# Rotated q and k as 16-bit halves, balanced by the norm weights; k transposed once, c spread by a transfer, and the list of instructions laid anew

## The chip, the cores and the metric

The kernel runs on one core of one Trainium2 chip. The metric is device time in microseconds (us) for one execution. The engines are named as the profile names them: PE (TensorE, with PEld for its weight loads), DVE (VectorE), ACT (ScalarE), POOL (GpSimd) and SP (SyncE, which here only issues transfers).

## The reference: one decoder layer with two mixers

The layer works on x (1 x 1024 x 1024, 32-bit). A conditioning row c gives shift, scale and gate; the normalised and modulated x goes through one input projection; its columns feed a sparse attention with three branches and a diagonal state-space mixer in parallel; both are gated, joined and projected back. Cut to what matters here:

```
mod = silu(c) @ w_ada + b_ada                       # shift, scale, gate
h = rms_norm(x, norm_g) * (1 + scale) + shift
q, kcr, vcr, ksl, vsl, kwn, vwn, z_a, g_br, u, z_s = split(h @ w_in)
q = rms_norm(q, q_norm_g)                           # 8 heads of 64
k_slc, k_win = rms_norm(ksl, k_slc_norm_g), rms_norm(kwn, k_win_norm_g)   # 2 groups of 64
q_r, k_slc, k_win = (apply_rope(v, cos, sin) for v in (q, k_slc, k_win))
# compressed branch: q (not rotated) against kc; selected and window branch:
s = einsum(q_r, k) * 64 ** -0.5;  p = masked_softmax(s);  o = p @ v
attn = (g0 * o_cmp + g1 * o_slc + g2 * o_win) * silu(z_a)
y = s5_mixer(u);  y = gelu(y);  ssm = y * sigmoid(y @ glu_w + glu_b) * silu(z_s)
out = x + gate * (concat(attn, ssm) @ w_out)
```

With 1024 positions and 16 selected blocks of 64, the selected branch takes all earlier keys; the window branch takes the last 512.

## The kernel before

**Recording and order.** The kernel first records every instruction under a short name and an engine letter, and then issues them in the order of a long list, `ORD`: `ha00:p5` means the next five PE instructions of the item `ha00` (letters p, v, a, g, s for PE, DVE, ACT, POOL, SP). Each engine keeps exactly this order, and takes its instructions strictly in turn. `SLOTS` gives each tile its buffer. All rows of the profile carry line L375, the helper that issues, so that instructions are told apart by their tiles.

**Start.** Row tiles of x are loaded, c is loaded as one row and spread over the 128 partitions by a matmul with ones (`sc_half`, line 528, tile `pcb`), SiLU is formed from it, and DVE multiplies and sums it with the rows of w_ada (`wada`, 24 times). DVE also forms the row norms, x is scaled, transposed by PE (`ptr`) and written as high and low part (`hhi`, `hlo`).

**Projections.** All products with 32-bit data are taken as three matmuls: high x high, high x low, low x high (`ptp` for k, v and q, `pcp` for the others).

**k.** `kv_norm` (line 768) normalises two row tiles of k, multiplies by the norm weights (`gains`) and by the rotary tables on DVE; `rope` (line 705) adds the halves on POOL and writes each head's 64 columns twice side by side (`kr`). `part2` (line 779) transposes the doubled heads on PE (`pkt`, 8 transposes for two row tiles), ACT copies the result (`kh`), and on the lower 64 partitions DVE subtracts it from the exact value: so the upper 64 rows hold k's high part and the lower 64 its low part. `kh` goes to DRAM (`kTd`) and comes back as `kT` (`kt`, line 1799), 128 partitions by 4 x 1024, 32 bits each.

**q.** `q_rope` doubles the rotated q in the same way; `q_trans` (line 1395) transposes it, ACT takes the high part `qh` (times 1/8), DVE the rest `ql`.

**Attention.** Blocks of 128 queries go in the order 0, 1, 2, 3, 7, 6, 5, 4, eight heads each. `head_a` (line 1452) takes the scores S of both branches: for `qh` and then `ql` as the stationary operand, kT streams through in pieces of up to 512 columns, so that the 128 rows sum high and low part of k; masks are added by a 16-bit matmul (`dmask`, `identb`). DVE finds the row maximum (`st`), ACT the exponential (`pp`); `head_b` on ACT writes the 16-bit high part of the weights (`hl`), `head_c` on DVE the low part, and SP's transposing transfer makes `PT`. `unit_b` multiplies PT by the values on PE (`po<-V,PT`, 64 columns each). In blocks 4 to 7 the selected branch has 640 to 1024 keys and the window branch 640; in blocks 0 to 3 both have 128 to 512.

**Beside it** PE has the state-space part, the gate projections (`pcp`), and behind them the output projection (`po<-wo`), which the list puts between the heads.

Of the kernel before, what the change touches and what calls it, by code (L numbers as in the profile page):

```python
# [75 lines left out]
cmpk:p2 tab0:v cmpk:p u3:a cmpk:p tab0:v cmpk:p qa0:p kpbn0:v scan0:v2 cmpk:p mats0:a u3:s cmpk:p2 tab1:v tab1:a cmpk:p
scan1:a cmpk:p2 scan0:a qa0:p2 mats0:a qa0:p scan0:v qa0:p2 mats1:p tab1:v mats1:p2 scan0:v mats1:p4 mats0:v mats1:p2
scan0:v mats1:p4 scan0:v mats1:p3 cmpk:p tab1:v cmpk:p2 mats1:a mats0:v cmpk:p tab1:v cmpk:p mats0:s mats1:a cmpk:p
mats1:p tab1:v mats0:s mats1:p3 scan0:v mats1:p3 mats1:a mats1:p mats0:s qa1:p scan0:v qa1:p mats1:a qa1:p2 xl2:s
mats1:a qa1:p2 mats0:s scan0:v cmpk:p mats1:a cmpk:p2 mats0:s mats1:a cmpk:p2 scan0:v cmpk:p mats0:s cmpk:p2 scan0:v  # L80
mats0:s scan1:p2 scan0:v scan1:p qaw4:s scan1:p scan0:v scan1:p mats0:s scan1:p2 scan0:v scan1:p scan1:a qaw3:s qa2:p2
scan1:a scan0:v qa2:p mats3:g qa2:p scan1:a qa2:p scan0:v qa2:p scan1:a cmpk:p scan1:v2 cmpk:p cmpk:a cmpk:p2 kpbn0:v
scan1:v cmpk:p2 cmpk:a cmpk:p cmpk:a scan1:v cmpk:p cmpk:a cmpk:p cmpk:a cmpk:p kpbn0:v cmpk:a scan0:v cmpk:p cmpk:a
cmpk:p cmpk:a cmpk:p kpbn0:v scan1:v cmpk:p3 scan1:v cmpk:p2 kpbn0:v qa0:p scan1:v qa0:p2 mats1:v qa0:p scan1:v qa0:p2
# [233 lines left out]
    pos="01",  # L318
# [1627 lines left out]
```

## Time and profile before

Three timed runs gave 638.22, 639.57 and 639.63 us. The profile is of one further execution.

| | |
|---|---|
| median of the timed runs | 639.57 us |
| time of the profiled execution | 643.35 us |
| its span, first to last instruction | 640.3 us |
| PE matmul busy | 604.2 us (94%) |
| PE weight loads busy | 488.4 us (76%) |
| DVE busy | 560.2 us (87%) |
| ACT busy | 377.6 us (59%) |
| POOL busy | 143.1 us (22%) |
| granted TensorE clock | 1.000 |

Busy time is the time in which at least one instruction of an engine is under way. Matmuls overlap each other, so a row's mean is longer than the time from one start to the next. A row of a group gives line, engine, operation, the tiles written and read, shapes, the count, then busy us and mean ns of one, then the idle time of the engine before them with what ended it. A row of the waits gives who waited for whom: us in total, times, longest. The timeline gives start, length, and what ran.

### The profile page before, as it was taken

The page shows a single profiled execution, that of the slowest core. Times are in us where ns is not written, and L with a number is a line of the kernel's source. Part 1 is how long each engine was busy: PE and PEld are TensorE (multiplying, and loading weights), DVE is VectorE, ACT ScalarE, POOL GpSimd, SP SyncE. Part 2 cuts the span into 40 slices and gives each one's busy share as a digit, 9 for nine tenths or more (in the row PEclk, how much of TensorE's full clock was granted, in tenths as well). Part 3 has the DMA queues.
Part 4 walks back from the last instruction along what each step waited for, and adds up shares of the span by engine and source line. Part 5 has one row for each costly group of instructions (what it writes and reads, how often), then busy time and mean ns, then how long its engine had stood idle before and what let it go on. Part 6 is the DMA issues. An engine that isn't in the chain of part 4 may idle for free.

```text
span 640.3 us, 12597 instructions
## 1 busy us (share of the span) xinstructions
PE 604.2 (94%) x4662; PEld 488.4 (76%) x4662; DVE 560.2 (87%) x1107; ACT 377.6 (59%) x732; POOL 143.1 (22%) x162
## 2 busy tenths in 40 slices
PE   2499999999999999999999999999999899999996
PEld 0388887888888887888888876657779788788884
DVE  5999988899878799898776879989999999999974
ACT  3596443755226325437677797786677677756750
POOL 1132225401873002170131011011120311201200
PEclk9999999999999999999999999999999999999999
DMA  8985325612869653063386979996999999999996
GB/s 316 398 311 119 100 66 162 190 39 50 219 166 279 187 133 101 18 168 126 99 161 166 171 161 240 175 221 219 204 205 179 221 209 215 238 218 239 234 174 197
DMA packets 209759, 116.75 MB, mean 182 GB/s; under 512 B 159073, under 2 KB 188513, under 8 KB 209698
## 3 DMA queue, kind: packets, MB, share of 16 engines
q1 hardware_dynamic: 205858, 109.38, 70.2%
q0 software_dynamic: 3840, 6.57, 4.7%
q8 instruction: 36, 0.59, 0.4%
q14 instruction: 25, 0.20, 0.1%
HBM read 58.10 MB, written 18.61 MB: 120 GB/s over the span
## 4 chain that ended last, share of the span: by engine, by line
PE 26%; DVE 11%; DMA 10%; issue 4%; ACT 3%; POOL 1%; SPq 0%; ACTq 0%; DVEq 0%; POOLq 0%
PE po L375 12%; PE S L375 6%; DMA PT<-hl 6%; PE pcp L375 5%; DVE hl L375 4%; DVE st L375 3%; DVE ps L375 1%; ACT pp L375 1%; DMA wor<-in_w_out_dram 1%; ACT hl L375 1%; DMA wr<-in_w_in_dram 1%; DMA yd<-Y 1%; DMA zz<-zsd 1%; PE pc L375 1%; POOL qr L375 1%
## 5 line engine op out<-in xcount | busy, mean ns | idle before, releaser
L375 ACT ACTIVATE pp<-S,st 128x640 f32<-128x640 f32 (+7 forms) x128 | 88.9, 698 | 48.0 <-DVE st L375 25.1
L375 ACT ACTIVATE hl<-pp,st 128x640 f16<-128x640 f32 (+7 forms) x128 | 90.0, 732 | 28.8 <-DVE st L375 13.1
L375 DVE SCALAR_TENSOR_TENSOR hl<-pp,st,hl 128x640 f16<-128x640 f32 (+7 forms) x128 | 97.6, 783 | 5.1 <-ACT hl L375 4.8
L375 DVE TENSOR_REDUCE st<-S 128x1 f32<-128x640 f32 (+7 forms) x96 | 84.3, 883 | 9.3 <-PE S L375 8.4
L375 PE MATMUL po<-wo,oh 128*128 128x512 f32 x264 | 83.6, 401 | 2.5 <-DVE ps L375 1.5
L375 PE MATMUL pcp<-hhi,wh 128*128 128x512 f32 x208 | 84.5, 406 | 0.4 <-DVE zz L375 0.2
L375 PE MATMUL ptp<-wsp,hhi 128*128 128x512 f32 x256 | 84.3, 410 | 0.0
L375 PE MATMUL pcp<-hlo,wh 128*128 128x512 f32 x208 | 82.3, 396 | 0.0
L375 PE MATMUL pcp<-hhi,wl 128*128 128x512 f32 x208 | 82.0, 394 | 0.0
L375 PE MATMUL S<-kT,qh 128*128 128x128 f32 (+3 forms) x192 | 60.8, 375 | 1.4 <-ACT pp L375 1.2
L375 PE MATMUL po<-V,PT 128*128 128x64 f16 x1584 | 58.6, 193 | 0.9 <-DMA PT<-hl 0.9
L375 PEld LDWEIGHTS po<-wo,oh 128*128 128x128 f32 x264 | 48.5, 188 | 14.3 <-ACT hl L375 1.8
L375 PEld LDWEIGHTS <-PT 128*128 128x128 f16 x1584 | 54.0, 98 | 3.5 <-issue 1.6
L375 PEld LDWEIGHTS ptp<-wsp,hhi 128*128 128x128 f32 x256 | 47.8, 193 | 10.6 <-issue 0.3
L375 PE MATMUL S<-kT,ql 128*128 128x128 f32 (+3 forms) x192 | 53.7, 338 | 0.0
L375 PE MATMUL ptp<-wsp,hlo 128*128 128x512 f32 x128 | 51.3, 402 | 0.0
L375 PE MATMUL po<-wo,ol 128*128 128x512 f32 x120 | 47.4, 395 | 0.0
L375 PEld LDWEIGHTS pcp<-hlo,wh 128*128 128x128 f32 x208 | 39.1, 188 | 9.3 <-issue 0.2
L375 PEld LDWEIGHTS pcp<-hhi,wh 128*128 128x128 f32 x208 | 39.2, 189 | 8.9 <-DVE zz L375 0.4
L375 PEld LDWEIGHTS pcp<-hhi,wl 128*128 128x128 f32 x208 | 39.2, 188 | 8.2 <-issue 0.2
L375 POOL TENSOR_TENSOR qr<-ropeb 128x512 f32<-128x512 f32 x16 | 21.8, 1381 | 96.3 <-DVE ropeb L375 56.1
L375 PEld LDWEIGHTS S<-kT,qh 128*128 128x128 f32 x192 | 33.2, 190 | 8.1 <-ACT pp L375 3.0
(310 smaller groups left out, 1264.2 us busy)
## 6 DMA issues: line engine op xcount, KB each, us to landing
wada<-in_w_adaT_dram SPq DMA_DIRECT2D x24, 512.0 KB, 6.8
wr<-in_w_in_dram SPq DMA_DIRECT2D x14, 512.0 KB, 5.2
x<-in_x_dram SPq DMA_DIRECT2D x8, 512.0 KB, 7.0
wor<-in_w_out_dram SPq DMA_DIRECT2D x8, 512.0 KB, 4.8
out_dram<-o SPq DMA_DIRECT2D x16, 256.0 KB, 2.8
wraw<-in_w_in_dram SPq DMA_DIRECT2D x15, 256.0 KB, 4.2
xo<-in_x_dram SPq DMA_DIRECT2D x14, 256.0 KB, 3.7
ud<-U SPq DMA_DIRECT2D x4, 512.0 KB, 3.3
```

Source lines behind the costliest of these rows:

```text
L375: op(*now(a), **{n: now(x) for n, x in k.items()})
```

## The change

- q's and k's rotated halves are written as 16-bit floats (F16) instead of 32-bit ones (F32R): `kh`, `kTd`, `kT`, `qh`, `ql`. The score matmuls keep their number and their columns.
- So that 16 bits hold them, `balance` measures the squares of the norm weights of q and k and multiplies one by a power of two and the other by its inverse: two ACT squares and a dozen small DVE operations on `gains`, ahead of all that uses them.
- `rope` writes k once instead of twice; `part2` transposes the plain heads (4 transposes for two row tiles), takes one copy (high) and one subtraction (low) over all 128 partitions, and stores both apart. `kt` puts high and low part on the upper and lower partitions as it loads.
- c is loaded by a transfer that writes its row to all 128 partitions; ones, `pcb` and their matmuls go.
- `ORD` and `SLOTS` are laid anew as a whole.

```
-prep0:g kvaw0:s xl_1:s s5l:s2 pre:s3 kvaw0:a pre:s2 kvaw0:g pre:s pre:v mb2:s s5p:v ma0:s sc0:p s5p:v2 lb:s s5p:v2 lb:s
...
-    cr = w4([1, 1024], F32, "cr")
-    dma(cr[:], t["c"].rearrange("(a d) -> a d", a=1))
+    cr = w4([128, 1024], F32, "cr")
+    dma(cr[:], t["c"].partition_broadcast(128))
...
-    ones = w2([1, 128], F32, "ones")
-    dve.memset(ones[:], 1.0)
...
-        pcb = ppv("pcb")
-        pe.matmul(pcb[:], ones[:], cr[:, halves(n)], start=True, stop=True)
-        act.activation(sc[:, halves(n)], pcb[:], AF.Tanh, scale=0.5)
-        stt(sc[:, halves(n)], sc[:, halves(n)], 1.0, pcb[:], OP.add, OP.mult)
+        act.activation(sc[:, halves(n)], cr[:, halves(n)], AF.Tanh, scale=0.5)
+        stt(sc[:, halves(n)], sc[:, halves(n)], 1.0, cr[:, halves(n)], OP.add, OP.mult)
...
+        balance(g)
         return cs, g
+
+    def balance(g):
+        junk = w2([128, 144], F32, "bj")
+        ss, v, w, n, f = (junk[:, 128 + 2 * k:130 + 2 * k] for k in range(5))
+        act.activation(junk[:, :64], g[:, 0, :], AF.Square, accum_out=ss[:, 0:1])
+        act.activation(junk[:, :128], g[:, 1:3, :].rearrange("p a d -> p (a d)"), AF.Square, accum_out=ss[:, 1:2])
+        ts(dve, v, ss.bitcast(I32), 2.0 ** -25, None, OP.mult)
+        for k, (top, off) in enumerate(((78.5, 1.0), (75.5, -1.0))):
+            ts(dve, w[:, k:k + 1], v[:, k:k + 1], -2.0, top, OP.mult, OP.add)
+            tt(dve, n[:, k:k + 1], v[:, 1 - k:2 - k], v[:, k:k + 1], OP.subtract)
+            stt(n[:, k:k + 1], n[:, k:k + 1], off, w[:, k:k + 1], OP.add, OP.min)
+        ts(dve, n, n, MAG, None, OP.add)
+        ts(dve, n, n, MAG, None, OP.subtract)
+        ts(dve, f.bitcast(I32), n, 8388608.0, 127.0 * 8388608.0, OP.mult, OP.add)
+        ts(dve, g[:, 0, :], g[:, 0, :], f[:, 0:1], None, OP.mult)
+        gk = g[:, 1:3, :].rearrange("p a d -> p (a d)")
+        ts(dve, gk, gk, f[:, 1:2], None, OP.mult)
...
         for h, op in ((0, OP.subtract), (1, OP.add)):
+            if m == 2:
+                tt(pool, o[:, :, 32 * h:32 * h + 32], c[:, :, h], b[:, :, 1 - h], op)
+                continue
...
-    kTd = dram.tile([128, 4, 1024], F32, name="kTd")
+    kTd = dram.tile([128, 2, 2, 1024], F16, name="kTd")
...
-        kr = w4([128, 8, 2, 64], F32, "kr")
+        kr = w4([128, 2, 8, 64], F32, "kr")[:, 0]
...
-            kh = w4([128, 4, 256], F32R, "kh")
-            for j in range(2):
-                pt = ppv("pkt")
-                for b in range(4):
-                    pe.transpose(pt[:, b * 128:(b + 1) * 128], kr[:, 4 * j + b].rearrange("p a d -> p (a d)"), ident[:])
-                pt4 = pt[:].rearrange("p (b t) -> p b t", b=4)
-                ks = kh[:, :, 128 * j:128 * j + 128]
-                act.copy(ks, pt4)
-                tt(dve, ks[64:128], pt4[64:128], f32(ks[64:128]), OP.subtract)
+            kh = w4([128, 2, 2, 256], F16, "kh")
+            pt = ppv("pkt")
+            for m in range(4):
+                pe.transpose(pt[:, m * 128:(m + 1) * 128], kr[:, 2 * m:2 * m + 2].rearrange("p g d -> p (g d)"), ident[:])
+            pt4 = pt[:].rearrange("p (j b t) -> p b j t", j=2, b=2)
+            hi, lo = (kh[:, n].rearrange("p b (j t) -> p b j t", j=2) for n in range(2))
+            act.copy(hi, pt4)
+            tt(dve, lo, pt4, hi, OP.subtract)
...
-        qh = w2([128, 4, 128], F32R, "qh")
-        ql = w2([128, 4, 128], F32R, "ql")
+        qh = w2([128, 4, 128], F16, "qh")
+        ql = w2([128, 4, 128], F16, "ql")
...
-        kT = Late(lambda: pa.tile([128, 4, 1024], F32R, name="kT"))
-        for n in range(2):
-            for b in range(4):
-                pool.dma_start(kT[:, b, halves(n)], kTd[:, b, halves(n)])
+        kT = Late(lambda: pa.tile([128, 4, 1024], F16, name="kT"))
+        for b in range(2):
+            for g in range(2):
+                for n in range(2):
+                    pool.dma_start(kT[64 * n:64 * n + 64, 2 * b + g, :], kTd[64 * g:64 * g + 64, n, b, :])
```

What the new list makes of it is read at two places. The first is DVE's list at the program's start. Before (`sm` are the state-space parameters, `sq` the squares of x, `sc` SiLU of c):

```order
L375 TENSOR_SCALAR sm_150<-s5p 128x16
L375 TENSOR_SCALAR sm_156<-sm_150 128x16
L375 TENSOR_SCALAR sm_156<-sm_156 128x16
L375 SCALAR_TENSOR_TENSOR sm_160<-sm_156,sm_150 128x16
L375 SCALAR_TENSOR_TENSOR sm_160<-sm_156,sm_160 128x16
L375 TENSOR_SCALAR sm_164<-sm_160 128x16
L375 TENSOR_TENSOR sm_164<-sm_164,sm_160 128x16
L375 TENSOR_SCALAR sm_164<-sm_164 128x16
L375 TENSOR_TENSOR sm_164<-sm_164,sm_160 128x16
L375 SCALAR_TENSOR_TENSOR sq,ss<-x_72 128x1024
L375 TENSOR_SCALAR sm_164<-sm_164 128x16
L375 SCALAR_TENSOR_TENSOR sc<-sc,pcb 128x512
```

And DVE's first rows in the changed kernel, from `cr`, the loaded c:

```order
L376 SCALAR_TENSOR_TENSOR sc<-sc,cr 128x512 x2
L376 TENSOR_SCALAR sm_150<-s5p 128x16
L376 TENSOR_SCALAR sm_152<-sm_150 128x16
L376 TENSOR_SCALAR sm_152<-sm_152 128x16
L376 SCALAR_TENSOR_TENSOR sm_157<-sm_152,sm_150 128x16
L376 SCALAR_TENSOR_TENSOR sm_157<-sm_152,sm_157 128x16
L376 TENSOR_SCALAR sm_161<-sm_157 128x16
L376 TENSOR_TENSOR sm_161<-sm_161,sm_157 128x16
L376 TENSOR_SCALAR sm_161<-sm_161 128x16
L376 SCALAR_TENSOR_TENSOR wada,macc<-wada,sc 128x1024
```

Both halves of SiLU of c have moved to the head of DVE's list, ahead of the state-space parameters, and the first sum with w_ada ahead of the first square of x.

The second place is PE's list at the selected branch of the first head of block 4 (640 keys). Before, with transposes of attention output (`pat`) in between:

```order
L375 LDWEIGHTS identb
L375 MATMUL S<-dmask,identb 128x128
L375 MATMUL pat<-ident,A 128x128 x4
L375 MATMUL S<-kT,qh 128x128
L375 MATMUL S<-kT,qh 128x512
L375 MATMUL S<-kT,ql 128x128
L375 MATMUL S<-kT,ql 128x512
```

The same branch on PE in the changed kernel:

```order
L376 LDWEIGHTS identb
L376 MATMUL S<-dmask,identb 128x128
L376 LDWEIGHTS qh
L376 MATMUL S<-kT,qh 128x128
L376 LDWEIGHTS qh
L376 MATMUL S<-kT,qh 128x512
L376 LDWEIGHTS ql
L376 MATMUL S<-kT,ql 128x128
L376 LDWEIGHTS ql
L376 MATMUL S<-kT,ql 128x512
L376 MATMUL po<-wo,oh 128x512 x2
```

The matmuls of S are the same in number and width; each 16-bit one has its weight load as an instruction of its own, and an output projection has taken the place of the transposes.

More of the change, by code (lines that the diff above doesn't have):

```diff
@@ L278 @@
[L278 to L282 removed]
+cmpK:g pre:s s5l:s2 mb0:s pre:s3 mb1:s sc1:a ma0:s lb:s sc0:a sc1:v pre:s sc0:v s5p:v3 ma4:s s5p:v2 pre:s s5p:v3 mb0:v
@@ new lines @@
+xb20:p mc2:v h40:a xb20:p rstd1:v xb20:p ma6:s ma3:v kva0:p3 h20:a kva0:p2 rstd1:v kva0:p h40:a rstd1:v ma7:s kva1:p
+mc3:v rstd1:v kva1:p rstd1:v kva1:p h20:a rstd1:v kva1:p mod1:s rstd1:v mc3:v kva1:p rstd1:v kva1:p rstd1:v h20:g
+xsc1:v xb30:p kvaw6:s kvaw2:a xb30:p3 u1m:p xsc1:v u1m:p h30:a u1m:p kvaw2:g xb50:p kvaw5:s xb50:p2 xsc1:a xb50:p
+u2m:p3 cmpv:s kva2:p ma5:v kva2:p xsc1:a kva2:p tb:s kva2:p3 mb5:v h30:a kva2:p3 kvaw3:a kva2:p2 h30:v mb7:s kvaw7:a
+kva2:p xb01:p kvaw3:v xb01:p3 tb:s u3m:p2 h40:v h01:a u3m:p kva3:p mc5:v kva3:p kvaw4:a kva3:p2 tb:s h01:a kva3:p
@@ new lines @@
+mats0:p qaw1:v mats0:p2 mats1:p3 mats0:a prep1:v mats1:p3 u3:a mats1:p2 prep1:v mats1:p4 qaw3:v kpat1:p2 u3:s kpat1:p2
+mats1:p prep0:v mats1:p ll:s mats1:p kpat1:a mats1:p cmpk:p2 tabf:v3 cmpk:p tab1:v mats1:a cmpk:p2 tabf:v mats1:a
+prep1:v cmpk:p qa0:p mats0:p tab0:v mats0:p3 cmpk:p kpat1:v cmpk:p mats0:a mats0:g cmpk:p2 scan0:a tab0:v kpat1:s
+scan0:p2 tab1:v scan1:a scan0:p2 tab0:v qa0:p2 tab0:v qa0:p scan0:a qa0:p tab0:v qa0:p tab0:a scan0:p scan0:a tab0:v
+scan0:p2 mats0:a scan0:v scan0:p mats1:p4 qa1:p scan0:a qa1:p2 mats1:a qa1:p scan0:v qa1:p scan0:a qa1:p mats0:v
@@ new lines @@
+mats2:s kpbt1:p hidk:p2 kpbt1:a out1:g hidk:p mats2:s hidk:p qp0:a hidk:p kpbt1:v tb:g hidk:p hidv:s hidk:p2 mats2:s
+mats2:p qp0:v mats2:p3 qa7:p2 mats2:a qa7:p2 prep3:v qa7:p cz0:s qa7:p hidv:p tab2:v hidv:p qp1:a hidv:p4 mats2:a
+hidv:p hidv:s qp1:v hidv:p mats2:a hidv:p kpbt1:s hidv:p2 cmpv:a hidv:p prep3:v mod5:s hidv:p2 mats2:s hidv:p qpn0:v
+hidv:p qpn0:v2 hidv:p mats2:s qpn0:v hidv:p qpn0:v hidv:p qpn0:v hidv:p mats2:s qpn0:v hidv:p qpn0:v hidv:p hidk:v
+qpn0:v hidv:p qpn0:v hidv:p qpn0:v hidv:p qpn0:v hidv:p3 qpn0:v hidv:p3 prep3:v qs0:s hidv:p qb0:p2 mod7:s hidk:v
@@ new lines @@
+prep3:g z0_1:p z0_7:v z0_1:p scan2:a z0_1:p2 scan2:a z0_1:p scan2:v qb2:p3 prep3:v qb2:p3 scan2:v yp01:s mats3:p3
+scan2:v mats3:p5 scan3:v mats3:p8 z0_2:p2 tab3:v z0_2:p mats3:a z0_2:p scan2:v z0_2:p yp01:a z0_2:p z0_3:p scan2:v
+mats3:a z0_3:p2 tab3:v hidk:a z0_3:p2 tab3:v z0_3:p qb3:p yp01:v qb3:p cz2:a qb3:p2 hidk:v scan2:v qb3:p2 tab3:a qb3:p
+hidk:v qb3:p cz1:a qr0:v qb3:p3 scan2:v cok:p z0_3:a cok:p gates:p3 cok:a scan2:v gates:p cmpK:a gates:p4 scan2:v
+gates:p2 scan2:v gates:p2 qb3:p scan2:v qb4:p3 z0_3:v qr0:g qb4:p3 mats3:p z0_7:s mats3:p qr0:g mats3:p2 gates:p2
@@ new lines @@
+scan3:v z1_4:p4 out2:p scan3:v out2:p2 scan2:v out2:p3 scan3:v out2:p2 qb6:p mats3:v qb6:p scan3:v z1_5:p mats3:s
+out2:a z1_5:p2 cmpK:v qt00:v mats3:s z1_5:p out2:g z1_5:p2 scan3:v out2:g mats3:s z1_6:p3 scan3:v out2:g mats3:s
+z1_6:p2 cmpK:v z1_6:p out2:g cmpK:v mats3:s out2:p cmpK:v2 scan3:v out2:p2 mats3:s out2:p cmpK:v hidv:v out2:p cmpK:v
+out2:p cmpK:v mats3:s ca0:p cmpK:v ca0:p cmpK:v ca0:p2 cmpK:v out2:p mats3:s cmpK:v out2:p kt:x qr1:v z1_7:p3 out2:a
+cmpK:v z1_7:p qpb0:v z1_7:p ca0:a z1_7:p out2:g cmpK:p qb6:p2 kt:g cmpK:a scan3:v qb6:p cmpK:a ca0:p out2:g scan3:v
@@ new lines @@
+ub45:p hb47:a ub45:p11 ub44:p12 ub43:p3 ub45:p3 hc47:v ub45:p5 ub43:a ub45:p13 ub44:p9 hc46:v ao60:p hc47:s ao60:p
+ub45:a ao60:p2 ao50:v ao60:p2 ub43:p hc46:s ub43:p ao61:p2 ub43:v ao61:p2 ao60:v ub43:a ao61:p2 hc47:s ub43:v ub45:p2
+ao61:v ub45:p3 ao60:v ub45:p2 ao61:v ub45:p ao60:s ub45:p2 ao70:v ao50:s ub45:p3 ao71:v ub46:p11 ub45:v ub46:p3 ao71:s
+ub46:p9 ub45:a ub46:p ub47:p4 ao51:s ub47:p2 ub46:p5 ub45:v ub46:p4 ub47:p3 ao70:s ub47:p14 ao61:s ub47:p12 ub47:a
+ub47:p5 ub47:v ub47:a ub47:v lo:p5 lo:v lo:p lo:v lo:g lo:v lo:s2
@@ L306 @@
-    sm="012034453463111616134714536",
-    pv="00010101010100011001000111001010000010111111100000000001101000101010100010",
+    w4=(
+        "012340567859AB6A2BCC41709D6EF6DG80HIE1CF0D6451EE2BEEAG8450I6GDFA19CHG572GGCHG4A1C75HC29I4HC572426D2D"
+        "2D92DDII729I4AD97G239EFI4B13B9D27A5DDA7H9EFA6C2C9BH15I4312GB15A3C7GHD9F3I6B21CA948GFD5B047E68I12AC53"
+        "B4HG6EF0IC95BHDG7102IACB53E68H49D1GFA3B7C024I80E15H93A8GB2ICDE6HF148B7906EIDHF83DCE52918A0G7DB149A3I"
+        "FBC2EH41IF0746DB3IHFG7A645180IDH29EFD7BG812H3CD5FG8476I2DH5B972G64AF80CB3D5I7HEAC940G8D24513FI690HC4"
+        "83EAIB7GFDC96H5AI8G34CB6EG178H052C4AIB60FD7GH9ABE3CF2548H69IDCE0B47A2"),
@@ L308 @@
+    sm="012034513564333360763764350",
+    w2=(
+        "01234523678709A39B5A69B8947C6694A1B25A32AB513C87B618C9257CB14C8194C675B72C982B61C45789A915B4308762CA"
+        "4B0296C819986537C0A1364C5BC79B753893125B188349C0A4024A266B85414107B93AB2452C9809783C6257A09601063254"
+        "782B59638105271A9A4A7B83B5C621B43608429846CA5274B8A12C78B44C249C942"),
     vtmp="01",
+    pv="01101010101010000101011011111001011111100000000000000001010101011010",
     S=(
-        "0101101011001011010101010101010100110100101010110010101010101010101010101010101101001010101010110110"
+        "0110101001010110101010101010001010101010010101010101001101010110101010101010101001010110010101101010"
@@ L311 @@
         "1010"),
     mm=(
-        "0100101010101010101000110110010110010010011000101010111010010100101011010010101010010011001010101001"
-        "01011100101"),
+        "0100010101010101001000110010010110101010001000101010110101111001010101010101010010101101101101101100"
+        "10101100101"),
+    pos="01",
+    b="0123231021",
+    a="0123332021232021030231",
     w2s="01",
-    b="0122331022",
-    a="0123331021123012031230",
-    pos="01",
     pbh="01",
     mc="01010101",
-    lc="01001010",
@@ L322 @@
-    st="01230123013201320132031023102310",
-    f2="01230345241232045034230543150452401425134053435453102503425130",
-    p4="01231320")
+    st="01231021302130210321032013202103",
+    lc="01010101",
+    f2="01232450540312302413521042453052101240525231423501305242031532",
+    p4="01230132")
 N4, N2, F2 = 19, 13, 6
@@ L713, in rope @@
         c, b = (cb_[:, k].rearrange("p (h s d) -> p h s d", h=8, s=2) for k in range(2))
-        two = lambda x, h: x[:, :, h, None, :].to_broadcast([128, 8, 2, 32])
         for h, op in ((0, OP.subtract), (1, OP.add)):
+            if m == 2:
+                tt(pool, o[:, :, 32 * h:32 * h + 32], c[:, :, h], b[:, :, 1 - h], op)
+                continue
+            two = lambda x, h: x[:, :, h, None, :].to_broadcast([128, 8, 2, 32])
             tt(pool, o[:, :, :, 32 * h:32 * h + 32], two(c, h), two(b, 1 - h), op)
@@ L779, in part2 @@
         def part2():
[L780 to L789 removed]
+            kh = w4([128, 2, 2, 256], F16, "kh")
[6 more added lines that the diff above has]
+            tt(dve, lo, pt4, hi, OP.subtract)
+            dma(kTd[:, :, :, i * 128:i * 128 + 256].rearrange("p n b t -> p (n b) t"),
+                kh[:].rearrange("p n b t -> p (n b) t"), "k")
         return part2
@@ L1401, in q_trans @@
             pe.transpose(pt[:, j * 128:(j + 1) * 128], qr[:, 2 * j + g].rearrange("p a d -> p (a d)"), ident[:])
-        qh = w2([128, 4, 128], F32R, "qh")
-        ql = w2([128, 4, 128], F32R, "ql")
+        qh = w2([128, 4, 128], F16, "qh")
+        ql = w2([128, 4, 128], F16, "ql")
         fl = lambda x: x[:].rearrange("p a b -> p (a b)")
         act.activation(fl(qh), pt[:], AF.Copy, scale=0.125)
-        stt(fl(ql), pt[:], 0.125, f32(fl(qh)), OP.mult, OP.subtract)
+        stt(fl(ql), pt[:], 0.125, fl(qh), OP.mult, OP.subtract)
         Q[i][g] = qh, ql
```

489 lines of the change are left out of this document (225 added, 264 removed).

## The prediction

> **What bounds the kernel now.** First the table of windows, the busy time of each engine by stretch of the program: projections and the state-space part up to about 280 us, blocks 0 to 3 of the attention to about 400, blocks 7 to 4 with the output projections behind them.
>
> ```profile
> 0.00:24.00 24.00, 4.14 (x4) 0.99 (x4) 17.54 (x58) 8.01 (x11) 1.99 (x6) 1.00 0.93 350
> 24.00:128.00 104.00, 103.20 (x491) 83.41 (x492) 93.58 (x271) 61.83 (x93) 37.01 (x37) 1.00 0.58 175
> 128.00:280.00 152.00, 150.66 (x905) 127.28 (x905) 133.60 (x256) 64.70 (x127) 45.10 (x66) 1.00 0.48 132
> 280.00:384.00 104.00, 101.70 (x701) 83.21 (x701) 82.28 (x177) 74.63 (x206) 20.37 (x24) 1.00 0.66 152
> 384.00:448.00 64.00, 62.59 (x609) 41.53 (x607) 60.24 (x93) 47.37 (x86) 7.63 (x6) 1.00 0.92 213
> 448.00:512.00 64.00, 61.48 (x634) 51.41 (x631) 61.07 (x86) 44.34 (x73) 11.45 (x9) 1.00 1.08 203
> 512.00:576.00 64.00, 62.58 (x683) 52.62 (x683) 62.22 (x94) 45.47 (x79) 10.85 (x8) 1.00 1.08 221
> 576.00:608.00 32.00, 32.00 (x342) 27.05 (x341) 29.88 (x49) 21.80 (x42) 6.19 (x5) 1.00 1.05 237
> 608.00:640.30 32.30, 25.81 (x312) 20.89 (x308) 19.79 (x32) 9.50 (x20) 2.55 (x2) 1.00 0.89 184
> ```
>
> Behind the length of each stretch stand PE, PEld, DVE, ACT and POOL, then the granted clock and the DMA share. From 24 us on a matmul is nearly always in flight: the PE column misses the window by 0.8, 1.3 and 2.3 us in the three rows up to 384. DVE misses it by 10.4, 18.4 and 21.7 us there. So PE sets the pace up to 384, and DVE has room. From 384 to 608 it is different: DVE's four rows add up to 213.4 of 224 us, 10.6 us idle, and PE's to 218.7. Two engines bind at once. The waits of DVE in that stretch say who makes it idle:
>
> ```profile
> DVE st L375 <- PE S L375: 3.5, 8, 1.0
> DVE hl L375 <- ACT hl L375: 1.6, 5, 0.6
> ```
>
> Only 3.5 us of its idle time ends with a score matmul (S), the work that this change makes cheaper. PE's own waits there are also short; the page gives for the whole run, per group, how long PE sat idle before the products with the transposed weights (PT), and the tile's view how long a transposing transfer takes to land:
>
> ```profile
> L375 PE MATMUL po<-V,PT 128*128 128x64 f16 x1584 | 58.6, 193 | 0.9 <-DMA PT<-hl 0.9
> DMA to landing us min/median/max: 2.3/4.0/7.0
> ```
>
> **The scores, the main term.** Each head takes its scores as q-high times k and q-low times k, k's rows holding high over low parts, now as 32-bit operands, then as 16-bit ones: the same columns, 384 matmuls before and after. The groups by form, and the two 16-bit forms that the run already has, 128 and 512 wide:
>
> ```profile
> L375 PE MATMUL S<-kT,qh 128*128 128x512 f32 x88 | 36.8, 433 | 0.0
> L375 PE MATMUL S<-kT,ql 128*128 128x512 f32 x88 | 35.5, 418 | 0.0
> L375 PE MATMUL S<-kT,qh 128*128 128x384 f32 x24 | 9.4, 393 | 0.0
> L375 PE MATMUL S<-kT,ql 128*128 128x384 f32 x24 | 8.1, 336 | 0.0
> L375 PE MATMUL S<-kT,qh 128*128 128x256 f32 x24 | 7.7, 336 | 0.0
> L375 PE MATMUL S<-kT,ql 128*128 128x256 f32 x24 | 6.4, 280 | 0.0
> L375 PE MATMUL S<-kT,qh 128*128 128x128 f32 x56 | 15.9, 291 | 1.4 <-ACT pp L375 1.2
> L375 PE MATMUL S<-kT,ql 128*128 128x128 f32 x56 | 12.9, 237 | 0.0
> L375 PE MATMUL S<-dmask,identb 128*128 128x128 bf16 x160 | 29.1, 224 | 1.8 <-ACT pp L375 1.2 <-DVE qn L375 0.6
> L375 PE MATMUL pc<-cmask,identb 128*128 128x512 bf16 x8 | 3.0, 379 | 0.0
> ```
>
> A pair of 512 goes from 433 + 418 to 2 x 379 ns, 93 ns less; a pair of 128 from 291 + 237 to 2 x 224, 80 less; between the two 16-bit forms by width, a pair of 384 goes to 655 (74 less) and one of 256 to 551 (65 less). That is 88 x 93 + 56 x 80 + 24 x 74 + 24 x 65 = 16.0 us. Means of pipelined matmuls overstate a single one, but a difference should hold; the timeline of one head of block 4 (640 keys, two branches) tests it by starts:
>
> ```profile
> 570.45 0.59 PE L375 MATMUL S<-kT,qh 128*128 128x128 f32 x2
> 570.88 0.50 PE L375 MATMUL S<-kT,ql 128*128 128x128 f32 x2
> 571.22 0.60 PE L375 MATMUL pat<-ident,A 128*128 128x128 f32 x4
> 571.73 0.61 PE L375 MATMUL S<-kT,qh 128*128 128x128 f32 x2
> 572.18 0.50 PE L375 MATMUL S<-kT,ql 128*128 128x128 f32 x2
> 572.53 0.28 PE L375 MATMUL S<-dmask,identb 128*128 128x128 bf16 x2
> 572.65 0.54 PE L375 MATMUL po<-V,PT 128*128 128x64 f16 x13
> ```
>
> Four score matmuls, 1280 columns, take 0.77 us (570.45 to 571.22) and 0.80 (571.73 to 572.53). The 16-bit products behind them come every (0.54 - 0.193) / 12 = 0.029 us for 64 columns, each with weights of its own, which makes 20 x 0.029 = 0.58 us for 1280: 0.19 to 0.22 less, where the form rows give 0.17. I keep 16.0.
>
> A wide 32-bit matmul already comes at the full rate; what falls away is mostly the loading of 32-bit weights behind a narrow one. The order now lists these loads apart; they cost nothing if they hide behind the matmul in flight, as the PT loads do.
>
> On TensorE, the Trainium skill ("TensorE: Matmul & The Clock Gate", The mechanism) says that a weight load overlaps matmuls in flight only where it goes to other rows of the array. By that rule 384 full-height loads would stand in line. The 29 ns per load and product above speak against it here; its result is the last rival.
>
> Where the 16.0 us fall, by PE's busy time on the tile S:
>
> ```profile
> 280.00:384.00 104.00, 26.44 (x174) 17.17 (x116) 21.07 (x28) 29.14 (x108) 1.00 0.66 152
> 384.00:608.00 224.00, 69.59 (x364) 42.67 (x264) 60.89 (x65) 66.05 (x142) 1.00 1.03 216
> ```
>
> About 27% (4.4 us) before 384, the rest, 11.6 us, behind. Up to 384 DVE has 21.7 us of room, so the 4.4 are taken whole. Behind 384 DVE can give up between the 3.5 us in which it waits for scores and all 10.6 of its idle time. I take 8: nearer the upper end, since a score set that ends earlier also moves up the exponentials on ACT, for which DVE waits as well (hl), and the new list may fill what is left. What is late next there is DVE, with work that the change leaves alone.
>
> **k transposed once.** Per pair of row tiles 4 transposes instead of 8, one copy and one subtraction instead of two.
>
> ```profile
> L375 PE MATMUL pkt<-ident,kr 128*128 128x128 f32 x32 | 4.8, 273 | 0.0
> L375 DVE TENSOR_TENSOR kh<-pkt,kh 64x512 fp32r<-64x512 f32 x8 | 5.6, 695 | 3.5 <-ACT kh L375 3.3
> L375 DVE TENSOR_SCALAR sm<-sm 128x16 f32<-128x16 f32 x15 | 2.6, 172 | 0.4
> ```
>
> PE: half of 4.8, 2.4 us at most; I take 2, on the pacing engine, in stretches where DVE has room. DVE: 4 x 0.695 = 2.8 us less, against 12 small operations of balance() at about 0.172, 2.1 us more, with two on ACT: nothing in sum, and hidden in the 28.8 us that DVE idles from 24 to 280. If that cover were gone it would be at most the 2.1. Balance adds a wait: both rotary tables (rq on POOL) and the gain products of k now come after its last scaling; behind rq on POOL stand block copies and the rotation of k, which the scores need only behind 280 us. POOL's rotations of k shrink too, off the path: its column in the table adds up to 143 of 640 us. The k traffic through DRAM halves as well; no row shows PE waiting for kT, so zero.
>
> **c by a transfer.** Before, a row of c was spread by matmuls:
>
> ```profile
> 3.48 0.62 ACT L375 CAST wsp<-wraw 128x512 fp32r<-128x512 f32 x1 [1.46 <-DMA wraw<-in_w_in_dram]
> 5.52 0.17 DVE L375 MEMSET ones<- 1x128 f32 x1 [5.52 <-POOL wsp L375]
> 24.10 0.69 PE L375 MATMUL ptr<-ident,x 128*128 128x128 f32 x2 [12.29 <-DVE x L375]
> wada<-in_w_adaT_dram SPq DMA_DIRECT2D x24, 512.0 KB, 6.8
> ```
>
> PE's real start at 24.10 waits for DVE's scaling of x, with 12.29 us idle before it. The pcb matmuls lie in time that PE has free, so their removal is worth nothing by itself. c becomes a transfer of 512 KB at the head of SP's queue, ahead of x and the weights; DVE's list now begins with its two products, which wait for it, and the queue behind (small operations, modulation sums, squares) waits along. In the empty queue the first 256 KB (wraw) reached ACT at 3.48 us; 512 KB in the filled queue take 6.8 from the issue, so c lands between 3.5 and 7.5. With 0.6 us of ACT behind it (as for wsp above) DVE begins between 4.1 and 8.1, where it began at 5.52: -1.4 to +2.6 us. I take 0.
>
> **The sum.** 4.4 + 8 + 2 + 0 = 14.4 us. The profiled execution has a span of 640.3 us and took 643.35, 3.8 us over the median of the three timed runs, 639.57; I take the gain off the median: 639.57 - 14.4 = 625.2 us. A measurement of this kernel can tell about 0.3%, 1.9 us, from no change.
>
> **The rivals.** *PE's whole gain arrives*: the list lets DVE work ahead before 384, where it idles 21.7 us, and 16.0 + 2 come through: 621.6 us, 620.2 with the early start. For it: DVE's idle time before 384 is larger than the whole gain. Against: DVE at 95% behind.
>
> *DVE holds the second half*: only 4.4 + 2 arrive, 633.2 us, or 635.8 with the late start. For it: just 3.5 of DVE's 10.6 idle us end with scores, and PE's weight loads (PEld) are busy only 172.6 of 224 us there, DVE 213.4. The Trainium skill ("Perfetto Trace Analysis", Identifying the Most-Contended Engine) judges TensorE by its weight loads and not by matmul busy time; by that rule VectorE alone binds from 384 on, and this rival's time would be the result. Against: PE's scores do end some of DVE's waits.
>
> *The 16-bit matmul saves nothing* beyond the 2 us of transposes, since a wide one costs 379 ns against 418 and the 39 may be an artefact of the eight cmask matmuls: 637.6 us, no change that can be told.
>
> *Slower, by the list*: PE takes its list strictly in turn. Behind 384 it now reaches the PT products up to 11.6 us earlier, while DVE, which makes their source (hl), cannot be that much earlier; 64 transposes of blocks 7 to 4 lie there, each landing in 2.3 to 7.0 us. If the new list puts their products too early by 0.3 us each (a tenth of the 3.0 between median and longest landing), PE loses 19.2 us and holds up the next scores, on which DVE waits: 639.57 - 14.4 + 19.2 = 644.4. It decides from 14.4 / 64 = 0.23 us each on. Against: 0.9 us of such waits now.
>
> *Slower, by weight loads in line*: 384 x 0.098 (the PT loads' median in the groups) = 37.6 us, against the 16.0 saved, less 2: 659.2.
>
> ```profile
> L375 PEld LDWEIGHTS <-PT 128*128 128x128 f16 x1584 | 54.0, 98 | 3.5 <-issue 1.6 <-DMA PT<-hl 1.2
> ```
>
> **How the numbers follow.** Forecast 0.48, whole gain 0.22, DVE holds 0.18, nothing saved 0.04, late PT 0.06, loads in line 0.02. Faster: 0.48 + 0.22 + 0.18 = 0.88; same 0.04; slower 0.08. The range runs from just under the whole gain with an early start (619) to DVE holding with a late one (636); it leaves out the last three rivals, 0.12, and a little beside them.
>
> **What would show it.** Right: score groups near 379 ns at 512 wide and 224 at 128; score sets of block 4 at about 0.6 us by starts; 16 pkt matmuls; the first ptr matmul within 22 to 26.6 us; DVE idle under 5 us in the stretch of blocks 7 to 4; the first scores of block 7 some 6 us earlier. Wrong: PE waiting for PT by more than a few us; score sets still at 0.77; DVE as idle as before in the second half while the end hardly moves.

## The result, and the profile after

The changed kernel takes 631.75 us (median of 4 runs, 630.28 to 634.17), the kernel before 639.33 (4 runs, 638.22 to 639.63): a ratio of 0.9888, 95% interval 0.9855 to 0.9922. So it is faster by 7.6 us (1.1%), where 14.4 were forecast; the direction and the range (619 to 636) held, the size was half. The profiled execution took 634.17 us with a span of 632.4.

The table of windows of the changed kernel, in the stretches that were used before (PE, PEld, DVE, ACT, POOL, then the granted clock, the DMA share and GB/s):

```profile
0.00:24.00 24.00, 0.00 (x0) 0.00 (x0) 17.21 (x54) 7.63 (x11) 0.54 (x6) 1.00 0.90 341
24.00:128.00 104.00, 97.33 (x431) 77.64 (x432) 89.47 (x273) 57.39 (x87) 33.72 (x35) 1.00 0.56 171
128.00:280.00 152.00, 151.13 (x926) 127.20 (x925) 126.32 (x243) 65.15 (x127) 46.44 (x70) 1.00 0.45 128
280.00:384.00 104.00, 103.61 (x740) 83.09 (x740) 90.70 (x205) 79.28 (x216) 18.26 (x23) 1.00 0.64 155
384.00:448.00 64.00, 61.79 (x593) 37.90 (x592) 59.47 (x88) 49.02 (x88) 10.12 (x8) 1.00 1.04 225
448.00:512.00 64.00, 60.91 (x667) 48.45 (x667) 61.19 (x94) 45.15 (x75) 9.62 (x8) 1.00 1.03 194
512.00:576.00 64.00, 61.52 (x661) 48.20 (x659) 60.09 (x92) 45.77 (x79) 13.45 (x11) 1.00 1.11 232
576.00:608.00 32.00, 29.71 (x392) 23.69 (x390) 29.50 (x49) 21.88 (x43) 4.62 (x4) 1.00 1.15 215
608.00:632.40 24.40, 17.91 (x241) 14.65 (x241) 13.95 (x24) 5.82 (x12) 1.69 (x2) 0.95 0.86 210
sum 632.40, PE 583.90 PEld 460.81 DVE 547.90 ACT 377.08 POOL 138.44; mean PE 64.88 PEld 51.20 DVE 60.88 ACT 41.90 POOL 15.38
```

PE is busy for 583.9 us, 20.3 less than the 604.2 before; 4.1 of these are the pcb matmuls, which lay in idle time. That leaves 16.2 us of work saved, close to the 18.0 of the forecast. But PE's idle time per stretch (length less PE column) tells where half of it went. From 24 to 128 us: 6.7, before 0.8, so 5.9 lost. From 128 to 384: 1.3, before 3.6, so 2.4 won. From 384 to 608: 10.1, before 5.3, so 4.7 lost. 16.2 - 5.9 + 2.4 - 4.7 = 8.0, the difference of the two spans (7.9). DVE is idle for 13.7 us from 384 to 608, before 10.6: it did not become the full engine.

The score groups by form, and k's transposes:

```profile
L376 PE MATMUL S<-kT,ql 128*128 128x512 f16 x88 | 32.1, 380 | 0.0
L376 PE MATMUL S<-kT,qh 128*128 128x512 f16 x88 | 32.1, 379 | 0.0
L376 PE MATMUL S<-kT,qh 128*128 128x128 f16 x56 | 11.6, 221 | 1.9 <-ACT pp L376 1.5 <-DMA kT<-kTd 0.4
L376 PE MATMUL S<-kT,ql 128*128 128x128 f16 x56 | 11.5, 219 | 0.0
L376 PE MATMUL pkt<-ident,kr 128*128 128x128 f32 x16 | 2.7, 279 | 0.0
```

379 and 220 ns, where 379 and 224 were forecast. One branch of a block-4 head by starts, 640 columns twice:

```profile
594.64 0.43 PE L376 MATMUL S<-kT,qh 128*128 128x128 f16 x2
594.91 0.43 PE L376 MATMUL S<-kT,ql 128*128 128x128 f16 x2
595.18 0.28 PE L376 MATMUL S<-dmask,identb 128*128 128x128 bf16 x2
```

0.54 us where it took 0.77. The saving is there; at the end of the program little of it is seen. PE's waits in the changed kernel, in order of size:

```profile
PE ptr L376 <- DVE x L376: 25.4, 2, 24.4
PE po L376 <- DMA PT<-hl: 4.1, 5, 1.4
PE ptr L376 <- ACT hf L376: 2.6, 1, 2.6
PE po L376 <- DMA PTc<-hlc: 2.3, 1, 2.3
PE S L376 <- ACT pp L376: 2.2, 3, 0.8
PE ptp L376 <- POOL wsp L376: 1.5, 1, 1.5
PE pu L376 <- DMA hlo<-hf: 1.3, 1, 1.3
```

Two kinds are new or larger: four waits at the start (1.0 of the first row, 2.6, 1.5, 1.3: the 6.7 us above with the last of the wait for x), and products that wait for transposing transfers (4.1 and 2.3; before 0.9 and 0).

### The profile page after: what moved, and what is told of

It is laid out like the page before. It is cut to its first block, busy times and chain, and to the rows that moved or that the text cites. A ratio compares the mean times of both kernels' runs of the same rounds, so it can differ in the third digit from the quotient of the medians.

```text
span 632.4 us, 12553 instructions
## 1 busy us (share of the span) xinstructions
PE 583.9 (92%) x4642; PEld 460.8 (73%) x4642; DVE 547.9 (87%) x1114; ACT 377.1 (60%) x732; POOL 138.4 (22%) x162
## 4 chain that ended last, share of the span: by engine, by line
PE 57%; DMA 14%; DVE 13%; issue 6%; ACT 4%; POOL 3%; SPq 3%; DVEq 0%; ACTq 0%; POOLq 0%
PE pcp L376 19%; PE po L376 11%; PE ptp L376 9%; PE S L376 6%; DMA PT<-hl 5%; SPq L376 3%; DVE hl L376 2%; DMA wada<-in_w_adaT_dram 2%; DMA PTc<-hlc 2%; DVE z L376 2%; PE pk L376 2%; DVE st L376 1%; DMA wor<-in_w_out_dram 1%; PE ph L376 1%; PE pc L376 1%
## 5 line engine op out<-in xcount | busy, mean ns | idle before, releaser
L376 ACT ACTIVATE hl<-pp,st 128x640 f16<-128x640 f32 (+7 forms) x128 | 88.5, 729 | 18.5 <-DMA PT<-hl 5.7
L376 DVE SCALAR_TENSOR_TENSOR hl<-pp,st,hl 128x640 f16<-128x640 f32 (+7 forms) x128 | 96.0, 777 | 3.3 <-ACT hl L376 3.2
L376 PE MATMUL po<-wo,oh 128*128 128x512 f32 x264 | 85.4, 410 | 1.0 <-ACT oh L376 0.8
L376 PE MATMUL po<-V,PT 128*128 128x64 f16 x1584 | 61.7, 194 | 4.2 <-DMA PT<-hl 4.1
L376 PEld LDWEIGHTS <-PT 128*128 128x128 f16 x1584 | 56.0, 98 | 12.3 <-DMA PT<-hl 5.6
L376 PE MATMUL S<-kT,qh 128*128 128x128 f16 (+3 forms) x192 | 48.5, 313 | 1.9 <-ACT pp L376 1.5
L376 PE MATMUL S<-kT,ql 128*128 128x128 f16 (+3 forms) x192 | 48.6, 313 | 0.0
L376 PE MATMUL ptr<-ident,x 128*128 128x128 f32 x64 | 10.8, 303 | 27.9 <-DVE x L376 25.4
```

What stands on the lines that cost most here:

```text
L376: op(*now(a), **{n: now(x) for n, x in k.items()})
```

## The experiments

Each kernel was timed in five rounds beside the kernel before on the same chip. Two theories stood at first. A: the type of the products brings the gain, the list's start gives part of it back. B: DVE holds the second half, and nothing that PE saves there counts.

**The changed kernel again, its type alone, its list alone.**

> The changed kernel once more, as the base for the runs beside it: 630 to 634 us (631.75 measured, 4 runs). In its trace PE idles 6.7 us between 24 and 128 us, where the kernel before idled 0.8.

Measured: 632.09 us, ratio 0.9881 (0.9855 to 0.9907).

```
-qh = w2([128, 4, 128], F16, "qh")        # ql, kh, kTd, kT alike
+qh = w2([128, 4, 128], F32R, "qh")
```

> The changed kernel with q's and k's rotated halves as 32-bit operands again (list, k transposed once, balance and c by a transfer stay). Theory A, the products' type brings the gain and the list's start gives part of it back: PE gets its 16 us of score time back, in part beside waits, so 643 to 648 us, slower than the kernel before. Rival B, the type is worth little because DVE holds the second half, and the list brings the gain: 632 to 636 us. Rival C, no list effect and whole type effect: 639 us less 2 for k, 637.

Measured: 640.38 us, ratio 1.0025 (0.9996 to 1.0053): the list and the rest without the type are worth nothing, or cost a little; not as slow as A said.

```
-qh = w2([128, 4, 128], F32R, "qh")       # ql, kh, kTd, kT alike, in the kernel before
+qh = w2([128, 4, 128], F16, "qh")
```

> The kernel before, list and all, with q's and k's rotated halves as 16-bit floats only (k still transposed twice, c by matmuls, no balancing by a power of two, so that small low parts lose bits). Theory A, PE binds up to 384 us and both engines behind: 4.4 us before 384 and 4 to 8 behind, 627 to 631 us, as fast as the changed kernel or faster. Rival B, DVE holds the second half: only the 4.4 us, 635 us. Rival C, the list brings the gain: 637 us or more.

Measured: 635.00 us, ratio 0.9932 (0.9909 to 0.9955). In the old list the type brings 4.1 us of its 16, in the new one 8.3 (e1 against e2). B's figure is met. The windows of e2, of e3 and of the changed kernel from 384 to 608 us:

```profile
384.00:608.00 224.00, 223.36 (x2298) 175.13 (x2297) 209.79 (x322) 161.86 (x284) 38.38 (x30) 1.00 1.04 217
```

```profile
384.00:608.00 224.00, 213.30 (x2288) 155.78 (x2287) 212.02 (x317) 159.81 (x279) 38.01 (x29) 1.00 1.07 216
```

```profile
384.00:608.00 224.00, 213.93 (x2308) 158.24 (x2306) 210.26 (x320) 161.82 (x282) 37.80 (x30) 1.00 1.07 217
```

With 32-bit products PE idles 0.6 us in that stretch, with 16-bit ones 10 to 11, in either list: much of what it saves there becomes idle time. DVE idles 12 to 14 us in all three, so "DVE is full" is not what the rows say either.

**The start.**

```
-kw0="p", kw2="p", h50="t"
+kw0="d", kw2="d", h50="d"
-kvaw0:g xsc0:v xb10:p2 ...  h00:a sq5:a mc1:v2 mb3:v h00:a ... kvaw2:g ... h50:g
+xsc0:v kvaw0:v xb10:p2 ...  h00:a h00:a sq5:a mc1:v2 mb3:v ... kvaw2:v ... h50:v
```

> The changed kernel with four places of the start altered: the low parts of two weight tiles (kvaw0, kvaw2) go from POOL to DVE, the square sq5 on ACT goes behind the second half of h00, and h50's low part comes from DVE in place of a transfer that adds. Theory A, the 5.9 us of PE idle time between 24 and 128 us pass to the end: PE idle there falls to 1 to 2 us and the time to 626 to 628 us. Rival B, DVE holds the second half, which absorbs an earlier PE: 630 to 632 us, with DVE less idle or PE more idle behind 384.

Measured: 627.88 us, ratio 0.9820 (0.9790 to 0.9850), 4.2 us below e1: the fastest of the kernels here that leave no work out. PE's row from 24 to 128 us, and DVE's scaling of x in it:

```profile
24.00:128.00 104.00, 102.46 (x480) 81.93 (x480) 95.96 (x289) 57.37 (x86) 32.25 (x34) 1.00 0.55 170
```

```profile
22.62 1.41 DVE L376 TENSOR_SCALAR x<-x,rstd 128x1024 f32<-128x1024 f32 x2
```

PE idles 1.5 us there in place of 6.7, and most of the difference passes to the end. In the changed kernel the same two scalings, beside POOL's part of a weight tile:

```profile
23.57 2.42 DVE L376 TENSOR_SCALAR x<-x,rstd 128x1024 f32<-128x1024 f32 x2
23.87 1.57 POOL L376 TENSOR_TENSOR wsp<-wraw,wsp 128x512 fp32r<-128x512 f32 x1 [22.94 <-ACT wsp L376]
24.37 0.69 PE L376 MATMUL ptr<-ident,x 128*128 128x128 f32 x2 [24.37 <-DVE x L376]
26.05 1.54 PE L376 MATMUL ptr<-ident,x 128*128 128x128 f32 x6 [0.98 <-DVE x L376]
30.16 1.11 PE L376 MATMUL ptr<-ident,x 128*128 128x128 f32 x4 [2.57 <-ACT hf L376]
```

DVE's pair takes 1.0 us longer while POOL's operation is under way, and the next transposes wait for it (0.98); then ACT takes the square ahead of hf, for which the following ones wait (2.57). The first start, at 24.37, tells nothing of this.

```
-sq2="d"  ... kvaw1:s sq2:v mb4:s
+sq2="a"  ... kvaw1:s sq2:a mb4:s         # on top of e4
```

> e4 with one more edit: the square sq2 of x goes from DVE to ACT, which waits there for its next tile. Theory, DVE's queue sets the first transposes: 1.2 us earlier (first at 22.2), and 1 us less at the end, 626 to 627.5. Rival, the transfers of x and w_ada set it: as e4, 627 to 628.5.

Measured: 628.84 us, ratio 0.9847 (0.9824 to 0.9871), no better than e4. The theory fell: the first transpose starts at 23.98 us, not at 22.2 (e4: 23.42). Two squares of x on ACT, on which the scaling of x depends, there end waits for transfers of x (2.72 and 2.60 us), which fits the rival.

```
-cr = w4([1, 1024], F32, "cr")            # and ones, pcb, their list entries, in the kernel before
+cr = w4([128, 1024], F32, "cr");  dma(cr[:], t["c"].partition_broadcast(128))
```

> The kernel before, list and all, with c spread by one transfer in place of the matmuls with ones; the transfer keeps c's place in the queue. Theory A, the transfer by itself costs nothing, and the 5.9 us at the start come from the list: 638 to 640 us, PE's first transposes within 1 us of 24.1. Rival, the 512 KB in the queue ahead of x delay x: 641 to 643 us, with the squares of x and the first transposes 2 to 4 us later.

Measured: 638.88 us against 638.04, ratio 1.0015 (1.0000 to 1.0030). The first transposes come 1.9 us later:

```profile
26.04 2.21 PE L375 MATMUL ptr<-ident,x 128*128 128x128 f32 x8 [26.04 <-DVE x L375]
```

At the end 0.8 us of it is seen. The time is theory A's and the late start nearly the rival's: the transfer brings nothing by itself and costs 0 to 2 us. The larger part of the loss at the start was the list's.

**Balance, and k's transposes.**

```
-        balance(g)                        # and its 14 list entries
```

> The changed kernel without the balancing by a power of two: its two squares on ACT and 12 small operations on DVE are gone, and the norm weights are used as they are. Theory A, they are hidden: 631 to 633 us. Rival, the waits that they add to DVE's and POOL's queues cost something: 628 to 630 us.

Measured: 631.35 us, ratio 0.9885 (0.9856 to 0.9915): hidden, as forecast.

```
-for m in range(4):
+for m in (0, 0, 1, 1, 2, 2, 3, 3):
```

> The changed kernel with each transpose of k issued twice (32 in place of 16; the second writes the same again). Theory A, PE sets the pace there and each costs what its start to start shows: 1 to 2.4 us more than the changed kernel's 632, 633 to 634.5. Rival, hidden beside waits: 631 to 633.

Measured: 631.78 us, ratio 0.9893 (0.9874 to 0.9913), against e1's 0.9881: 0.8 us more by the ratios, but the intervals overlap and leave room for nothing as for the whole 2 us. Whether the 2 us of k's transposes arrive can't be told from this.

**What holds the second half.**

```
-c1 = min(W, c0 + 512)
+c1 = c0 + 64 if i >= 4 and qx is ql else min(W, c0 + 512)
```

> The changed kernel, but in blocks 4 to 7 the products with q's low part take 64 columns of each piece in place of up to 512 (the rest of the low part's sum is left out): 38912 columns less for PE behind 384 us, about 17 us at the 224 ns of 128 columns less overlap (0.055 us by starts). DVE, ACT and the transfers keep their work. Theory A2, DVE and the chain through it hold the second half: the time falls by 0 to 3 us (629 to 632) and PE's idle time behind 384 grows by 13 us or more. Rival, PE holds it: 615 to 618 us.

Measured: 630.63 us, ratio 0.9886 (0.9862 to 0.9910): 17 us less for PE behind 384 (its busy time on S there falls from 58.9 to 42.0) and no gain. PE does not hold it.

```
-dve.tensor_reduce(out=st[br], in_=us[br][0][:, :W], ...)
+dve.tensor_reduce(out=st[br], in_=us[br][0][:, W - 192:W - 128], ...)   # and q scaled by 0.0125
```

> The changed kernel, but in blocks 4 to 7 DVE takes the row maximum over 64 columns in place of all 640 to 1024 (q is scaled down by ten so that the exponentials stay finite; the result is another softmax). About 43000 elements of a row less for DVE, some 50 us by its rows of 0.81 us for 640. PE keeps all its work. Theory A2, DVE and the chain through it hold the second half: the time falls by 8 to 14 us (618 to 624), until PE's list is full again (PE idle behind 384 from 10 us to under 3). Rival, PE holds it: 630 to 632 us.

Measured: 627.93 us, ratio 0.9841 (0.9816 to 0.9866): 44 us less for DVE on S (61.7 to 17.4) and 2.6 us gained against e1, with intervals that overlap, where 8 to 14 were expected. DVE does not hold it alone.

> Short maximum and narrow low scores together, in blocks 4 to 7 of the changed kernel (both leave work out, as in e5 and e6). Theory A2, DVE with the chain through it comes first behind 384 us and PE is full right behind it: with DVE relieved PE's 17 us count again, so 612 to 620 us, 8 us or more below e6's 627.9. Rival, something else holds both (the transposing transfers, ACT): 625 to 628 us, no less than e6.

Both edits together. Measured: 630.24 us (625.38 to 631.93), ratio 0.9882 (0.9859 to 0.9904). Relieving both brings no more than relieving DVE alone, so A and B both fall for this half. The profile is of the quickest of the seven executions, 625.38 us, 4 below the next one. Its row, and its first scores of block 7:

```profile
384.00:608.00 224.00, 207.53 (x2404) 156.06 (x2400) 176.44 (x322) 161.62 (x282) 38.19 (x29) 1.00 1.09 224
400.13 0.59 PE L376 MATMUL S<-kT,qh 128*128 128x512 f16 x2
```

PE idles 16.5 us, DVE 47.6, ACT 62.4; only the DMA share stands at its top. That column read 1.03 before the change too. So the third theory, D:

```
-sp.dma_start_transpose(PT[:, :2 * nk, :], hl[:, :2 * W])
+sp.dma_start_transpose(PT[:, :nk, :], hl[:, W:2 * W])                   # on top of e9, blocks 4 to 7
```

> e9 (narrow low scores and short maximum in blocks 4 to 7), and there the transposing transfers also carry only the low half of the weights, so half the size each (their number, place and source stay; the products take the low half twice, so the attention's result is not the reference's). Theory D, the transfers hold the second half, where the DMA share stands at 1.01 to 1.19: with them halved PE's 17 and DVE's 45 us count, PE's idle time behind 384 falls from 22 to under 8 us, 610 to 617 us. Rival, the waits between the engines (ACT's order, buffers) hold it: 626 to 631 us, as e9.

Measured: 614.58 us (612.51 to 617.09), ratio 0.9632 (0.9607 to 0.9656), 15.7 us below e9 and inside D's 610 to 617; between the two profiled executions it is 12.9. The row and the first scores of block 7:

```profile
384.00:608.00 224.00, 214.77 (x2529) 163.61 (x2524) 183.59 (x337) 162.84 (x288) 40.42 (x31) 1.00 0.85 182
400.95 0.59 PE L376 MATMUL S<-kT,qh 128*128 128x512 f16 x2
```

From these scores to the end of the span e9 takes 223.5 us, about as long as e6 (223.9), and e12 209.8. D's other sign was met only in part: PE's idle time from 384 us to the end fell from 22.4 to 11.9 us, not to under 8. The transposes held most of what the other two edits had set free, not all.

The number of transfers, their place and the tile that they read are the same; each carries half as much. The view of the DMA queues between 400 and 600 us, in the changed kernel and then in e12 (packets, MB, share of 16 engines' time; under it the issues and the median time to landing):

```profile
q1 hardware_dynamic: 115385, 42.96, 105.8%
...
PT<-hl SPq DMA_TRANSPOSE x64, 4.4
```

```profile
q1 hardware_dynamic: 82853, 35.16, 83.8%
...
PT<-hl SPq DMA_TRANSPOSE x72, 3.4
```

The share adds up the packets' times, which overlap, so it can pass 100%. In e9 it is 107.8%, with 4.6 us to landing, and before the change it was already 100.5%, with 4.4. With fewer packets the transposes land about 1 us earlier than in e9, and 72 of them fit into the stretch in place of 66.

## Why the prediction was right in direction and wrong in size

The direction follows from the scores, which did become cheaper. That the time fell inside the range is in part luck: the range reached that far up for "DVE holds the second half", which the runs do not bear out, and the measured gain is made up of other terms than the forecast's.

- **The scores, 16.0 us.** Right. e1 against e2 and the form rows show the groups' saving as sized. The 379 of the eight cmask matmuls was a fair price, so "saves nothing" falls. "Weight loads in line" falls too, and with it, for these loads, the rule that it was taken from: in e1 four products, each with its own weights, start 0.055 to 0.06 us apart, which leaves no room for 0.098:

```profile
288.00 0.22 PE L376 MATMUL S<-kT,qh 128*128 128x128 f16 x1
288.06 0.22 PE L376 MATMUL S<-kT,ql 128*128 128x128 f16 x1
288.12 0.22 PE L376 MATMUL S<-kT,qh 128*128 128x128 f16 x1
288.17 0.22 PE L376 MATMUL S<-kT,ql 128*128 128x128 f16 x1
```

- **4.4 us before 384.** Right in kind: the type's gain comes ahead of block 7. Its first scores, in the kernel before, in the changed kernel, in e2 (32 bits, new list) and in e1 (16 bits, new list):

```profile
407.10 0.71 PE L375 MATMUL S<-kT,qh 128*128 128x512 f32 x2
403.78 0.59 PE L376 MATMUL S<-kT,qh 128*128 128x512 f16 x2
408.66 0.71 PE L376 MATMUL S<-kT,qh 128*128 128x512 f32 x2
400.98 0.59 PE L376 MATMUL S<-kT,qh 128*128 128x512 f16 x2
```

From e2 to e1 they come 7.7 us earlier, of 8.3 in all. The old list gains 4.1 in all (e3). The new one gains more than the scores before 384 are worth, because with 32-bit k it also waits for k's way through DRAM, which the prediction set to zero. In e2:

```profile
289.54 0.38 PE L376 MATMUL S<-kT,qh 128*128 128x128 f32 x1 [2.02 <-DMA kT<-kTd]
```

That wait, with the slow clock behind it (below; 3.5 us at 0.51, so about 1.7 us lost, an estimate) and the 4.4, adds up to 8.1. In the changed kernel, with the transfers half as large, the wait is 0.4 us. A wait that no row of before shows can stand in a new list.

- **8 us behind 384.** This is the step that failed: "Two engines bind at once", and from it 8 of 11.6 us. Nothing of it arrived that can be measured. From block 7's first scores to the end of the span e2 takes 229.1 us with 32-bit products, the changed kernel 228.6 and e1 230.8 with 16-bit ones. (The kernel before takes 233.2 in its profile, which lies 3.8 us over its median, and e7, with the old list too, 229.9.) 17 us more off PE brought no gain either (e5). The sign named for it, DVE idle under 5 us, stayed out: 13.7. The other sign came in part: block 7's first scores stand 3.3 us earlier than before in the changed kernel and 6.1 in e1, where 6 were forecast, but by e2 what follows them is not shorter for the type. The rival "DVE holds the second half" had the better time, 633.2, and the wrong holder (e6, e9). The holder of that half, once PE and DVE are relieved, is the transposing transfers, by e12. That they also take the changed kernel's own gain is argued from PE's new waits for PT and PTc, 5.0 of its 10.1 idle us from 384 to 608, and from e5; halving them in the changed kernel alone was not tried. A sign of it stood in the last but one column of the table that the prediction quoted: DMA share 0.92, 1.08, 1.08 and 1.05 behind 384, against 0.48 to 0.66 from 24 to 384. The prediction read the engines' columns and passed over it. The Trainium skill ("Perfetto Trace Analysis", Identifying the Most-Contended Engine) advises to judge DMA by the use of memory bandwidth (HBM) and not by occupancy, which 16 engines make misleading, and then to find which DMA resource binds. The 217 GB/s that all transfers move here would not have raised suspicion, since the start moves 341; the share over 1.0 was the better sign here, with packets of 372 bytes on average (42.96 MB in 115385).

- **k once, 2 us.** Open: 0.8 us by e10, with intervals that leave room for 0 as for 2. **Balance, 0.** Right (e8).

- **The start, 0 us (-1.4 to +2.6).** Wrong by the list: 5.9 us of new idle time, of which e4 wins 4.2 back. The term looked only at the first transpose, which came at 24.37, 0.27 later, as forecast; the waits behind it came from POOL's and ACT's new order, which stands in the list and which the prediction did not follow.

- **Late PT in the list.** It came in a small way: PE's waits for PT rose from 0.9 to 4.1 us, 0.05 us for each of 64 transposes, far under the 0.23 from which it decides; one of 2.3 for PTc came in.

## What to carry to other kernels

Before a saving on one engine is booked in a stretch, read every column of that stretch's row, DMA share included: a column at its top before the change may be the bound, and then the saving turns into idle time beside it, as here. To find the holder, shorten one resource at a time and then several together; in the second half only the third edit here moved the time by more than the intervals. When an instruction list is laid anew, follow the critical engine for some microseconds behind its first start, since the start itself can stand still while the next three slip.

## What was not expected of the hardware

Two scalings of x on DVE take 1.41 us alone (e4) and 2.42 beside one POOL operation of 1.57. The Trainium skill ("SBUF — State Buffer", SBUF: two separate sides) says that VectorE, in some of its modes or with two inputs from SBUF, and GpSimd take a shared pair of ports in turn, each for a whole instruction. The rows fit: the pair ends at 25.99, 0.55 us behind the end of POOL's operation at 25.44. Which mode the scalings ran in, no row shows.

In e2 the granted clock falls to about half for 3.5 us right behind the 2.02 us wait for kT, so that the wait seems to cost more than itself (one trace):

```profile
289.50:293.00 3.50, 3.46 (x18) 3.40 (x18) 2.03 (x4) 1.81 (x9) 0.00 (x0) 0.51 1.05 379
```

The gap of 2.57 us before 30.16 in the changed kernel has a clock of 1.00 behind it (30.2 to 35.9 us), so the length of a pause alone does not decide. What does, no run here shows.

Halving the size of the transposing transfers lowered their median time to landing from 4.6 us (e9) to 3.4 (e12), and that of their issue on SP from 1.84 to 1.23. Whether the packets on the 16 engines, the issue on SP's queue or the delay of each transfer between one head's steps is what holds the half, no run here separates.
